# One Trainium2 core, a hybrid attention layer with 32 experts: half of the second matrix's columns computed from split weights, with the products of each unit in another order

## The chip, the cores and the metric

One core of one Trainium2 chip runs the whole layer as one program. The metric is device time in microseconds, from the first to the last instruction with what lies around them; a kernel's number is the median of its runs. PE stands for TensorE, PEld for its weight loads, DVE for VectorE, ACT for ScalarE, POOL for GpSimd, SP for SyncE.

## The reference, cut to what matters

The layer normalises 1024 tokens of width 1024, runs two kinds of attention heads, adds the result to the tokens, normalises again and sends each token to 4 of 32 experts. Only the experts are touched by the change (and the path by which `gate2`, a row of 1024 factors, reaches them):

```python
def expert_block(args):
    xe, e = args
    gu = xe @ w_gate_up[e] + b_gate_up[e]
    g = jnp.minimum(gu[:, :D_FF], SWIGLU_LIMIT)
    u = jnp.clip(gu[:, D_FF:], -SWIGLU_LIMIT, SWIGLU_LIMIT)
    act = (u + 1.0) * (g * jax.nn.sigmoid(SWIGLU_ALPHA * g))
    return act @ w_down[e] + b_down[e]
...
y = yb[dest] * gate_sorted[:, None].astype(yb.dtype)
...
return x + gate2 * y
```

All operands are float32. `w_gate_up[e]` is 1024 x 2048, `w_down[e]` 1024 x 1024.

## The kernel before, in words

**Order of the experts.** After attention and routing (until about 739 us) a loop handles the 32 experts one by one. A table `CAPS` gives the number C of token columns of each, 200 down to 96, by the rank of its load; the order sets one of 172 first, then one of 136, then wide ones (over 128, two blocks of rows) and narrow ones (128 or fewer, one block) in turn.

**Weights.** An expert's weights come in 12 chunks of 512 x 512 (1024 KB each), all issued on SP in the order of use (`load_chunk`, L775): eight of `w_gate_up`, four of `w_down`. Gate/up chunks go into a pool of five buffers (`eraw`, `NRAW`), `w_down` chunks into one of four (`draw`, `ND`). A gate/up chunk is *split* in two halves (`split_half`, L787): ACT copies 128 x 1024 values into a rounded float32 form (the *high* part, `hb`, 12 buffers, L796), and DVE subtracts that from the raw values into bfloat16 (the *low* part, `ha`, 6 buffers of two halves, L797). The subtraction stands right behind its copy.

**Products of the gate/up part** (`first_products`, L1157). The tokens are held as high and low columns side by side (`xx`, at least 256 columns) and as bfloat16 (`xb`). A *unit* is 512 columns of weights over the whole depth, two chunks: 32 high products of max(256, 2C) columns (L1167) and 32 low products of C columns in bfloat16 (L1171). They go 16 high, 16 low (first chunk), 8 high, 8 low, 8 high, 8 low (second chunk). An expert has four units: gate, up, gate, up. After each, ACT reads the low sums with the bias (L1179), DVE adds the high sums (L1183, L1181), ACT and DVE apply the sigmoid, the limits and the product (L1197, L1198, L1207, L1208), leaving `aa`.

**Products of `w_down`** (L1212 to L1229). Raw float32 weights times raw float32 `aa`: the profile shows two PE instructions for each such product, so a chunk is 32 instructions of C columns, and an expert 128. Between the two halves of the depth, PE transposes the next expert's gathered tokens (`stage_t`, L1131), which ACT, DVE and POOL copy into `xx` and `xb` (L1148, L1149, L1150). At the end ACT writes `yT` (L1225).

**The way back.** `back` (L1231) runs one step into the next expert: PE transposes `yT`, DVE multiplies by the token's weight and `gate2` (L1239), POOL scatters the rows with addition (L1153).

**What sets the order.** PE, ACT, DVE and SP run in the order in which the program is written here. `done(c)`, called when a chunk's products are issued, releases its buffers and calls `pump`, which issues every load that has a buffer, and one half split after a gate/up chunk, two after a `w_down` chunk, at most 12 halves ahead (`NH`). PSUM is eight single banks taken in turn (`bank`, L1095).

**gate2** is computed early (`mod_row`, L361) and kept as a broadcast 128 x 1024 tile.

Of the kernel before, what the change touches and what calls it, by code (L numbers as in the profile page):

```python
# [9 lines left out]
F32 = mybir.dt.float32  # L10
# [48 lines left out]
ND = 4  # L59
# [7 lines left out]
TB = 2  # L67
# [6 lines left out]
NC_ = 512  # L74
# [3 lines left out]
def hybrid_layer(ctx: ExitStack, tc: tile.TileContext, x, c_t, w_ada, b_ada_t, b_ada, norm1_t, w_in,  # L78
# [11 lines left out]
    modd = dram.tile([3, D], F32, name="modd")  # L90
# [30 lines left out]
    def rsqrt_mean(*a):  # L121
# [18 lines left out]
    gate2 = consts.tile([P, D], F32, name="gate2")  # L140
# [4 lines left out]
              [(w_down, n, kh) for kh in range(2) for n in range(2)]  # L145
    NGU, NCH = 8, len(CHUNKS0)
# [37 lines left out]
    with ExitStack() as st:  # L184
        with ExitStack() as sp:
# [164 lines left out]
            def mod_row(n, acc):  # L350
# [169 lines left out]
        with ExitStack() as so:  # L520
# [139 lines left out]
            m2 = rt.tile([P, 2, KT], F32, name="m2")  # L660
            wr = rt.tile([P, KT, E], F32, name="wr")
# [101 lines left out]
            at_ = {"dma": 0, "split": 0, "use": 0, "open": 0}  # L763
            raws, held = {}, {"eraw": 0, "draw": 0}
            pools = {"eraw": (wraw, NRAW)}
# [6 lines left out]
            def kind_of(d):  # L772
                return "eraw" if d % NCH < NGU else "draw"

            def load_chunk():  # L775
                d, kind = at_["dma"], kind_of(at_["dma"])
                i, w, n, kh = CHUNKS[d]
# [3 lines left out]
                raws[d] = pools[kind][0].tile([P, 4, NC_], F32, name=kind, bufs=pools[kind][1])  # L781
                nc.sync.dma_start(raws[d], w[ds(e, 1), kh * 512:(kh + 1) * 512, n * NC_:(n + 1) * NC_]
                                  .rearrange("o (k p) n -> p (o k) n", p=P))
                held[kind] += 1
                at_["dma"] += 1

            def split_half():  # L787

                t = at_["split"]
                c, q = t // 16 * NCH + t % 16 // 2, t % 2  # L790
                raw = raws[c][:, 2 * q:2 * q + 2]
                h_ = slot(False).rearrange("p (k n) -> p k n", k=2)
                if q == 0:
                    parts[c] = [], slot(True).bitcast(BF16).rearrange("p (k n) -> p k n", k=4)
                l_ = parts[c][1][:, 2 * q:2 * q + 2]
                nc.scalar.activation(h_, raw, AF.Copy)  # L796
                nc.vector.tensor_tensor(l_, raw, h_.bitcast(F32), OP.subtract)  # L797
                parts[c][0].extend((h_[:, j], l_[:, j]) for j in range(2))
                if q:
                    raws.pop(c)  # L800
                    held["eraw"] -= 1
                at_["open"] += 1
                at_["split"] += 1

            def pump(more):

                limit = min(at_["split"] + more, E * 16)
                while True:
                    d, t = at_["dma"], at_["split"]
                    kind = kind_of(d)  # L810
                    if d < len(CHUNKS) and kind in pools and held[kind] < pools[kind][1]:
                        load_chunk()
                    elif t < limit and t // 16 * NCH + t % 16 // 2 < d and at_["open"] < NH:
# [209 lines left out]
            pump(SPL[0] - at_["split"])  # L1023
# [6 lines left out]
            pump(SPL[1] - at_["split"])  # L1030
            pump(SPL[2] - at_["split"])
# [3 lines left out]
            pump(SPL[3] - at_["split"])  # L1035
            cur.places()
            pump(SPL[4] - at_["split"])
            cur.listed()
            pump(SPL[5] - at_["split"])
            cur.scattered()  # L1040
            pump(SPL[6] - at_["split"])
# [378 lines left out]
```

## Time and profile before

| | |
|---|---|
| runs | 2163.01 to 2168.81 us, median 2164.36 (3 runs) |
| the profiled execution | 2167.32 us, its span 2165.5 us |
| busy in the span | PE 97%, PEld 90%, DVE 69%, ACT 53%, POOL 20% |
| granted TensorE clock | 0.989 over the span |
| loads of expert weights | 256 of `eraw`, 128 of `draw`, 1024 KB each |

The experts' stage, 739 to 2153 us, is two thirds of the span, and all that follows concerns it but for a few lines. A busy PE says little by itself, since its matmuls overlap; how long a run of products takes is read from the start of one run to the start of the next in the timeline, and whether PE waited for anything from the list of waits.

### The profile page before, as it was taken

What the parts mean: (1) busy time and instruction counts of PE and PEld (TensorE: products, weight loads), DVE (VectorE), ACT (ScalarE), POOL (GpSimd) and SP (SyncE); (2) the same over time, 40 slices, a digit from 0 to 9 for tenths busy, and PEclk for the clock granted to TensorE, in tenths of its full rate; (3) what the DMA queues carried; (4) which work ended last, traced back from release to release, by engine and by line L of the source; (5) the groups of instructions that cost most, each with busy time, mean ns of one, the idle gap of its engine ahead of it and who ended that gap; (6) DMA issues with size and microseconds to landing.
All of it is one profiled execution on the core that took longest, in us unless ns stands there. A gap on an engine that the chain in (4) does not pass through costs nothing. (4 is left out here: it accounts for less than half of the span.)

```text
span 2165.5 us, 43655 instructions
## 1 busy us (share of the span) xinstructions
PE 2094.8 (97%) x16922; PEld 1957.5 (90%) x16922; DVE 1499.6 (69%) x2946; ACT 1150.2 (53%) x2263; POOL 429.3 (20%) x444
## 2 busy tenths in 40 slices
PE   7999999999999699999999999999999999999997
PEld 6877778998777699999999999999999999999997
DVE  6587756776666876677667677776767767667763
ACT  3522224777633455566456565656556656656652
POOL 2255532111045401111011111110111101101100
PEclk9999999999999799999999999999999999999999
DMA  7267886442224598799799999989989989999882
GB/s 294 73 163 215 221 230 172 114 109 76 89 105 153 192 356 299 247 334 350 255 292 326 300 314 319 332 312 343 315 297 312 361 297 320 323 315 335 297 320 60
DMA packets 272404, 548.98 MB, mean 254 GB/s; under 512 B 30675, under 2 KB 30691, under 8 KB 272067
## 3 DMA queue, kind: packets, MB, share of 16 engines
q1 hardware_dynamic: 250323, 490.09, 65.4%
q0 software_dynamic: 21872, 56.08, 11.1%
q8 instruction: 134, 2.20, 0.4%
q14 instruction: 75, 0.61, 0.1%
HBM read 501.31 MB, written 44.77 MB: 252 GB/s over the span
## 5 line engine op out<-in xcount | busy, mean ns | idle before, releaser
L797 DVE TENSOR_TENSOR ha<-eraw,hb 128x1024 bf16<-128x1024 f32 x512 | 601.3, 1224 | 233.5 <-ACT hb L796 233.0
L1167 PE MATMUL gu<-xx,hb 128*128 128x256 f32 (+13 forms) x4096 | 641.5, 304 | 0.6 <-DVE xx L1149 0.6
L1167 PEld LDWEIGHTS gu<-xx,hb 128*128 128x128 f32 x4096 | 561.1, 190 | 1.0 <-DVE xx L1149 0.8
L796 ACT ACTIVATE hb<-eraw 128x1024 fp32r<-128x1024 f32 x512 | 506.7, 1053 | 34.1 <-DMA eraw<-in_w_gate_up_dram 34.0
L1220 PE MATMUL gu<-aa,draw 128*128 128x128 f32 (+19 forms) x4096 | 521.2, 288 | 0.0
L1220 PEld LDWEIGHTS gu<-aa,draw 128*128 128x128 f32 x4096 | 511.2, 191 | 0.6
L1171 PE MATMUL gu<-xb,ha 128*128 128x128 bf16 (+19 forms) x4096 | 316.2, 224 | 0.0
L1179 ACT ACTIVATE tb<-gu,bcol 128x128 f32<-128x128 f32 (+19 forms) x512 | 164.6, 371 | 253.8 <-PE gu L1171 225.7
L1171 PEld LDWEIGHTS <-ha 128*128 128x128 bf16 x4096 | 246.6, 98 | 28.4 <-issue 3.3
L1153 POOL DMA_INDIRECT out_dram<-y,slot x47 | 81.6, 1736 | 528.3 <-DVE y L1239 251.4
L1126 POOL DMA_INDIRECT xg<-h2d,slot x47 | 54.5, 1160 | 629.0 <-PE gu L1146 381.8
L1225 ACT ACTIVATE yT<-gu,bcol 128x128 f32<-128x128 f32 (+19 forms) x256 | 82.4, 374 | 126.6 <-PE gu L1220 126.5
L572 DVE CUSTOM_DVE_ANT_0 p<-pss,bias 128x1024 f32<-128x1024 f32 (+7 forms) x128 | 94.4, 755 | 49.5 <-ACT p L581 22.2
L606 PE MATMUL po<-vsb,pT 128*128 128x64 f32 (+1 forms) x864 | 111.1, 275 | 2.6 <-ACT pT L600 1.5
L606 PEld LDWEIGHTS po<-vsb,pT 128*128 128x128 f32 x864 | 105.6, 194 | 4.8 <-ACT pT L600 1.8
L581 ACT ACTIVATE p<-p,mn 128x1024 f32<-128x1024 f32 (+7 forms) x128 | 98.6, 773 | 12.8 <-DVE mn L572 12.1
L1197 ACT ACTIVATE sg<-gt 128x256 f32<-128x256 f32 (+19 forms) x128 | 55.8, 436 | 89.2 <-DVE gt L1183 89.2
L461 PE MATMUL pp<-wh,hb 128*128 128x512 f32 x240 | 101.7, 424 | 0.0
L1198 DVE TENSOR_TENSOR gt<-gt,sg 128x256 f32<-128x256 f32 (+19 forms) x128 | 57.4, 448 | 63.4 <-ACT sg L1197 63.4
L112 POOL TENSOR_TENSOR rrs<-vrs,nhalf 128x8 f32<-128x8 f32 (+2 forms) x48 | 66.6, 1386 | 165.3 <-DVE vrs L110 160.2
L463 PE MATMUL pp<-wl,hb 128*128 128x512 f32 x240 | 94.9, 395 | 0.0
L462 PE MATMUL pp<-wh,hb 128*128 128x512 f32 x240 | 94.8, 395 | 0.0
(265 smaller groups left out, 2623.6 us busy)
## 6 DMA issues: line engine op xcount, KB each, us to landing
eraw<-in_w_gate_up_dram SPq DMA_DIRECT2D x256, 1024.0 KB
draw<-in_w_down_dram SPq DMA_DIRECT2D x128, 1024.0 KB
wraw<-in_w_ada_dram SPq DMA_DIRECT2D x32, 512.0 KB
wraw<-in_w_in_dram SPq DMA_DIRECT2D x23, 512.0 KB
hb<-in_w_ada_dram SPq DMA_DIRECT2D x16, 512.0 KB
qd<-tt POOLq DMA_DIRECT2D x32, 256.0 KB, 4.0
kd<-tt POOLq DMA_DIRECT2D x32, 256.0 KB, 4.2
ha<-qd SPq DMA_DIRECT2D x32, 256.0 KB
```

Source lines behind the costliest of these rows:

```text
L461: nc.tensor.matmul(pp, hh[b][:, k], wh[:, kk], start=(k == 0), stop=False)
L462: nc.tensor.matmul(pp, hl[b][:, k], wh[:, kk], start=False, stop=False)
L463: nc.tensor.matmul(pp, hh[b][:, k], wl[:, kk], start=False, stop=(k == KT - 1))
L572: nc.vector.tensor_tensor_reduce(p[:, :n], pss[:, :n], bias[:, (NB - 1 - ib) * P:(NB - 1 - ib) * P + n], -1.0, 3.0e38, OP.add, OP.min, mn)
L581: nc.scalar.activation(p, p, AF.Exp, bias=self.mn[c], scale=-1.0, accum_out=self.l[:, c:c + 1])
L606: nc.tensor.matmul(self.po[:, :w], self.pT[:, k], vsb[self.br][:, k, self.h * w:(self.h + 1) * w], start=(k == 0), stop=(k == self.ib))
L796: nc.scalar.activation(h_, raw, AF.Copy)
L797: nc.vector.tensor_tensor(l_, raw, h_.bitcast(F32), OP.subtract)
L1167: nc.tensor.matmul(pg[j][:, :max(256, 2 * C)], w[k][0][:, j * P:(j + 1) * P], xx[4 * kh + k], start=(kh + k == 0), stop=False)
L1171: nc.tensor.matmul(pg[j][:, C:2 * C], w[k][1][:, j * P:(j + 1) * P], xb[:, 4 * kh + k], start=False, stop=(kh == 1 and k == 3))
L1179: nc.scalar.activation(t, p[:, C:2 * C], AF.Identity, bias=bias, scale=1.0)
L1220: nc.tensor.matmul(p, w[:, k, j * P:(j + 1) * P], a[:, 4 * kh + k], start=(kh + k + j % 2 == 0), stop=(kh == 1 and k == 3 and j % 2 == 1))
```

## The change

Of the four `w_down` chunks of an expert the two of the first 512 output columns stay raw float32 (*plain*), and the two of the other 512 columns are split like gate/up chunks and computed as a fifth unit, with `a` itself as high, low and bfloat16 operands (`ax`, `ab`). So an expert has 20 half splits where it had 16. Split chunks share a ring of six buffers, plain ones have two. In each unit all 32 high products now come ahead of all 32 low ones, and the high parts' buffers are released ahead of the low ones'. The low part of a half is subtracted one half later than its copy. How many halves are split by each of the 14 steps of an expert is written out in `TG`. The transposes of the next expert's tokens stand in two places, after each plain chunk. PSUM is taken in four tiles of two banks. `gate2` is multiplied into the results while they are still transposed, as a column per partition (`g2c`), so that the way back is one ACT copy with the token's weight; it is loaded through a fourth row of `modd`. The diff, cut to its core:

```diff
-ND = 4
+NRING = 6
+NPL = 2
+TG = (12, 14, 16, 17, 19, 20, 22, 23, 24, 26, 27, 28, 28, 32)
...
-              [(w_down, n, kh) for kh in range(2) for n in range(2)]
-    NGU, NCH = 8, len(CHUNKS0)
+              [(w_down, n, kh) for n in range(2) for kh in range(2)]
+    NCH = len(CHUNKS0)
+    PLAIN = (8, 9)
...
-                    if v == 3:
-                        nc.vector.tensor_add(gate2[:, cs], pb, bb)
-                        return
                     nc.vector.tensor_add(bb, pb, bb)
...
+                nc.sync.dma_start(g2c, modd[3].rearrange("(k p) -> p k", p=P))
...
+            def low(t):
+                c, q = chunk_of(t)
+                nc.vector.tensor_tensor(parts[t][1], raws[c][:, 2 * q:2 * q + 2], parts[t][0].bitcast(F32), OP.subtract)
...
             def split_half():
...
-                nc.scalar.activation(h_, raw, AF.Copy)
-                nc.vector.tensor_tensor(l_, raw, h_.bitcast(F32), OP.subtract)
+                nc.scalar.activation(h_, raws[c][:, 2 * q:2 * q + 2], AF.Copy)
+                if t:
+                    low(t - 1)
...
-        def bank():
-            return ps4.tile([P, 512], F32, name="gu", bufs=8)
+        def banks():
+            return ps4.tile([P, 2, 512], F32, name="gu", bufs=4)
...
+        def done(high=0, low=0):
+            spent[0] += high
+            spent[1] += low
+            i, q = divmod(event[0], len(TG))
+            event[0] += 1
+            pump(i * NSP + TG[q])
...
+        def products(C, x, t0):
+            _, xb, xk = x
+            pg = [banks() for _ in range(2)]
...
             for kh in range(2):
-                c, w = take()
-                for js in ((0, 1), (2, 3)) if kh else ((0, 1, 2, 3),):
...
+                for j in range(4):
+                    for k in range(4 * kh, 4 * kh + 4):
+                        nc.tensor.matmul(pg[j // 2][:, j % 2, :max(256, 2 * C)], w[k][0][:, j * P:(j + 1) * P], xk[k],
+                                         start=(k == 0), stop=False)
                 if kh == 0:
-                    done(c)
+                    done(high=2)
+            for j in range(4):
+                for k in range(KT):
+                    nc.tensor.matmul(pg[j // 2][:, j % 2, C:2 * C], w[k][1][:, j * P:(j + 1) * P], xb[:, k],
+                                     start=False, stop=(k == KT - 1))
...
             for kh in range(2):
+                raw = raws.pop(d0 + kh)
+                for j in range(4):
+                    for k in range(4):
+                        nc.tensor.matmul(place(j), raw[:, k, j * P:(j + 1) * P], a[:, 4 * kh + k],
+                                         start=(kh + k + j % 2 == 0), stop=(kh == 1 and k == 3 and j % 2 == 1))
+                    if j == 1:
+                        f = slice(4 * kh, 4 * kh + 4)
+                        nc.scalar.activation(ah[:, f, :C], a[:, f], AF.Copy)
+                        nc.vector.tensor_sub(ah[:, f, C:], a[:, f], ah[:, f, :C].bitcast(F32))
+                        nc.gpsimd.tensor_copy(ab[:, f], ah[:, f, :C].bitcast(F32))
+                        done()
+                freed["p"] += 1
...
+                done()
+                between(kh)
+            pg = products(C, s_a, t0 + 16)
+            for j in range(4):
+                f, p = 4 + j, pg[j // 2][:, j % 2]
+                t = ap_.tile([P, 2, C], F32, name="tb", bufs=2)[:, 0]
+                nc.scalar.activation(t, p[:, C:2 * C], AF.Identity, bias=bc[:, 2 * KT + f:2 * KT + f + 1], scale=g2c[:, f:f + 1])
+                nc.vector.scalar_tensor_tensor(yT[:, f], p[:, :C], g2c[:, f:f + 1], t, op0=OP.mult, op1=OP.add)
+            done(high=2, low=4)
...
-                        nc.vector.scalar_tensor_tensor(y[:n, cs], py[:n], sl[:n, 1:2], gate2[:n, cs],
-                                                       op0=OP.mult, op1=OP.mult)
+                    nc.scalar.activation(y[:n].rearrange("p (k c) -> p k c", k=KT), py[:n], AF.Copy, scale=sl[:n, 1:2])
...
+        gate2 = fp.tile([P, D], F32, name="gate2")
+        nc.sync.dma_start(gate2, bcast_rows(modd, 3 * D, D))
```

The sums of the gate and up parts, the sigmoid and the product also go by wider tiles (two or four blocks of C columns in one DVE or ACT instruction where there were one or two).

## Rows read from the trace of the kernel before

**Rows 1.** Windows: stretch and length us; busy us of engines; clock, DMA share, GB/s.

```profile
739.20:2152.50 1413.30, 1412.65 (x13072) 1378.60 (x13072) 985.06 (x1628) 816.59 (x1503) 187.88 (x207) 1.00 0.90 307
...
1074.80:1115.70 40.90, 40.90 (x419) 40.18 (x417) 30.09 (x52) 25.30 (x48) 6.03 (x7) 1.00 0.91 294
1074.80:1198.70 123.90, 123.90 (x1235) 121.44 (x1233) 92.52 (x152) 75.52 (x142) 19.56 (x20) 1.00 0.96 311
1500.00:1520.00 20.00, 20.00 (x195) 19.66 (x195) 11.70 (x18) 10.54 (x22) 3.74 (x4) 1.00 1.05 387
```

**Rows 2.** Waits of PE in 743 to 2152 us: total, times, longest us.

```profile
PE gu L1167 <- DVE xx L1149: 0.6, 1, 0.6
```

**Rows 3.** Timeline of PE, an expert of 128 columns: start us, length us, what.

```profile
1082.31 2.15 PE L1167 MATMUL gu<-xx,hb 128*128 128x256 f32 x16
1084.31 1.07 PE L1171 MATMUL gu<-xb,ha 128*128 128x128 bf16 x16
1085.19 1.19 PE L1167 MATMUL gu<-xx,hb 128*128 128x256 f32 x8
...
1088.12 2.15 PE L1167 MATMUL gu<-xx,hb 128*128 128x256 f32 x16
...
1099.75 7.36 PE L1220 MATMUL gu<-aa,draw 128*128 128x128 f32 x64
1106.95 1.63 PE L1146 MATMUL gu<-ident,xg 128*128 128x128 f32 x16
```

**Rows 4.** The same view, an expert of 188 columns.

```profile
1028.82 2.98 PE L1167 MATMUL gu<-xx,hb 128*128 128x376 f32 x16
...
1037.07 2.98 PE L1167 MATMUL gu<-xx,hb 128*128 128x376 f32 x16
...
1053.62 10.38 PE L1220 MATMUL gu<-aa,draw 128*128 128x188 f32 x64
1063.83 1.04 PE L1146 MATMUL gu<-ident,xg 128*128 128x128 f32 x8
```

**Rows 5.** The same view, the last expert, of 96 columns.

```profile
2126.25 2.15 PE L1167 MATMUL gu<-xx,hb 128*128 128x256 f32 x16
...
2131.66 2.15 PE L1167 MATMUL gu<-xx,hb 128*128 128x256 f32 x16
...
2137.09 14.50 PE L1220 MATMUL gu<-aa,draw 128*128 128x96 f32 x128
2151.42 1.14 PE L1237 MATMUL gu<-ident,yT 128*96 128x128 f32 x8
```

**Rows 6.** Groups in 1074.8 to 1115.7 us: busy us, mean ns, idle before and releaser.

```profile
L797 DVE TENSOR_TENSOR ha<-eraw,hb 128x1024 bf16<-128x1024 f32 x16 | 18.7, 1220 | 7.7 <-ACT hb L796 7.7
...
L796 ACT ACTIVATE hb<-eraw 128x1024 fp32r<-128x1024 f32 x16 | 15.8, 1055 | 0.0
...
L1179 ACT ACTIVATE tb<-gu,bcol 128x128 f32<-128x128 f32 x16 | 5.0, 360 | 6.4 <-PE gu L1171 5.2 <-DVE ut L1181 1.2
...
L1198 DVE TENSOR_TENSOR gt<-gt,sg 128x256 f32<-128x256 f32 x4 | 1.7, 425 | 1.9 <-ACT sg L1197 1.9
...
L1239 DVE SCALAR_TENSOR_TENSOR y<-gu,slot,gate 128x512 f32<-128x512 f32 x2 | 1.4, 744 | 0.0
...
L1149 DVE TENSOR_TENSOR xx<-gu,xx 128x512 fp32r<-128x512 f32 x2 | 1.3, 686 | 1.4 <-ACT xx L1148 1.4
```

**Rows 7.** Lines 797 and 1150: shortest, median and longest instruction ns; times.

```profile
L797 DVE TENSOR_TENSOR ha<-eraw,hb x512: 1207/1219/3003, 730.2 to 2129.1; 128x1024 bf16<-128x1024 f32 x171
...
L1150 POOL CAST xb<-xx x98: 202/592/1685, 741.0 to 2106.2; 128x512 bf16<-128x512 f32 x40, 128x496 bf16<-128x496 f32 x6, 128x176 bf16<-128x176 f32 x4, 128x32 bf16<-128x32 f32 x4
```

**Rows 8.** Timelines of DVE and of POOL around 1192 us.

```profile
1191.42 4.14 DVE L797 TENSOR_TENSOR ha<-eraw,hb 128x1024 bf16<-128x1024 f32 x2
...
1192.70 1.78 POOL L1150 CAST xb<-xx 128x512 bf16<-128x512 f32 x4
```

**Rows 9.** Timeline of SP around 302 us.

```profile
302.55 0.37 SPq L618 DMA_DIRECT2D m<-modd  x1
```

More of the change, by code (lines that the diff above doesn't have):

```diff
@@ L89, in hybrid_layer @@
     ovd = dram.tile([P, 2], I32, name="ovd")
-    modd = dram.tile([3, D], F32, name="modd")
+    modd = dram.tile([4, D], F32, name="modd")
     tmp = ExitStack()
@@ L762, in hybrid_layer @@
             parts, reg = {}, {0: 0}
-            at_ = {"dma": 0, "split": 0, "use": 0, "open": 0}
-            raws, held = {}, {"eraw": 0, "draw": 0}
-            pools = {"eraw": (wraw, NRAW)}
+            at_ = {"dma": 0, "split": 0}
+            raws, pair = {}, []
+            pools = {0: (wraw, NRAW, "eraw")}
+            taken, freed = {"s": 0, "p": 0}, {"s": 0, "p": 0}
+            spent = [0, 0]
             def expert_of(i):
@@ L772, in kind_of, with room @@
             def kind_of(d):
-                return "eraw" if d % NCH < NGU else "draw"
+                return "p" if d % NCH in PLAIN else "s"
+            def room():
+                d = at_["dma"]
+                if d == len(CHUNKS):
+                    return None
+                k = kind_of(d)
+                if taken[k] - freed[k] == (NRING if k == "s" else NPL):
+                    return None
+                return pools.get("p" if k == "p" else int(taken[k] % NRING >= NRAW))
             def load_chunk():
-                d, kind = at_["dma"], kind_of(at_["dma"])
-                i, w, n, kh = CHUNKS[d]
+                d = at_["dma"]
+                pool, n, name = room()
+                i, w, c, kh = CHUNKS[d]
                 e = expert_of(i)
@@ L797, in split_half @@
-                nc.vector.tensor_tensor(l_, raw, h_.bitcast(F32), OP.subtract)
[L798 to L802, printed above, removed]
+                if t % 2 == 0:
+                    pair.append(slot(True).bitcast(BF16).rearrange("p (i k n) -> p i k n", i=2, k=2))
+                parts[t] = h_, pair[-1][:, t % 2]
+                nc.scalar.activation(h_, raws[c][:, 2 * q:2 * q + 2], AF.Copy)
@@ L803, in split_half, with pump @@
+                if t:
+                    low(t - 1)
                 at_["split"] += 1
-            def pump(more):
-                limit = min(at_["split"] + more, E * 16)
+                if t == E * NSP - 1:
+                    low(t)
+            def pump(upto):
                 while True:
-                    d, t = at_["dma"], at_["split"]
-                    kind = kind_of(d)
-                    if d < len(CHUNKS) and kind in pools and held[kind] < pools[kind][1]:
+                    if room():
@@ new lines, in expert, with joined @@
+        def expert(i, st, between):
+            C, bc = st["C"], st["bc"]
+            a = ap_.tile([P, KT, C], F32, name="ay")
+            s_a = operand(C, "ax", "ab")
+            t0, d0 = i * NSP, i * NCH + PLAIN[0]
+            def joined(dst, p, f, more):
+                t = ap_.tile([P, 2, C], F32, name="tb", bufs=2)
+                for j in range(2):
+                    nc.scalar.activation(t[:, j], p[:, j, C:2 * C], AF.Identity, bias=bc[:, f + j:f + j + 1], scale=1.0)
+                if more:
+                    nc.vector.scalar_tensor_tensor(dst, t, more, p[:, :, :C], op0=OP.add, op1=OP.add)
+                else:
+                    nc.vector.tensor_add(dst, p[:, :, :C], t)
@@ L1231, in back @@
+            pg = products(C, s_a, t0 + 16)
[4 more added lines that the diff above has]
+                nc.vector.scalar_tensor_tensor(yT[:, f], p[:, :C], g2c[:, f:f + 1], t, op0=OP.mult, op1=OP.add)
+            done(high=2, low=4)
             def back():
-                for (t0, n), sl in zip(st["blocks"], st["slots"]):
+                for (r0, n), sl in zip(st["blocks"], st["slots"]):
@@ L1309, in hybrid_layer @@
             nxt = stage_g(i + 1) if i + 1 < E else None
[L1310 removed]
+            expert(i, st, lambda g: nxt and stage_t(nxt, g))
             st = nxt
```

187 lines of the change are left out of this document (77 added, 110 removed).

## The prediction, made from the rows above

> **What bounds the kernel now.** I read the windows first: in the experts' stage PE is busy for 1412.65 of 1413.30 us while DVE is busy for 985 and ACT for 817, at the full granted clock [rows 1]. As busy matmuls overlap, I then read the waits: from 743 us on PE waited for another engine once, for 0.6 us [rows 2]. So the stage is as long as PE's own list of products, and the timeline gives the length of each piece from start to start [rows 3 to 5]. Last come the two things that could take PE's place: the vector engines (in a narrow expert of 40.9 us DVE is busy 30.1 us and ACT 25.3) and the transfers (a mean share of 0.90 at 307 GB/s over the stage, 0.96 at 311 GB/s in a stretch of three experts of at most 140 columns) [rows 1].
>
> **What PE loses and gains.** An expert gives up half of its plain instructions, 64, and gets one more unit, 32 high and 32 low products. At 128 columns the 64 plain ones take 1106.95 - 1099.75 = 7.20 us and a unit 1088.12 - 1082.31 = 5.81 us: 1.39 us saved [rows 3]. At 188 columns it is 10.21 against 8.25, 1.96 saved [rows 4]. In the last expert, 96 columns, half of 2151.42 - 2137.09 is 7.17 and a unit 5.41: 1.76 saved [rows 5]. The plain products do not get shorter below 128 columns (7.20 and 7.17) while the unit does, and above 128 they grow faster than it does. Reading all 32 experts so, from the first (1.18 us) to the last (1.76), gives 1.2 to 2.0 us each and 48 us in all: **-48**, between -46 and -50 by the spread of repeated units.
>
> The order inside a unit: a run of 16 high products takes 2.00 us and one of 16 low ones 0.88, and twice both makes 5.76, while the unit of six runs took 5.81 [rows 3]. A unit now has one run of each kind instead of three, so about 0.05 less in each of 5 x 32 units, if a run of 32 is twice one of 16. Not all of that need come: **-4**, between 0 and -10. The transposes only change place: the same number, 0.
>
> **What the evacuation must now keep up with.** The last up unit's results (`a`, second half) used to be covered by two plain chunks and the transposes, 7.2 + 1.6 us, and now by one chunk, 3.6 us, and some 0.4 us of transposes. What must fit in: two more ACT readings of 0.36, then two DVE sums and their limits and products of about 0.43 each [rows 6], some 2 us after the unit's end. With up to two half splits of 1.2 us queued ahead on DVE it takes 4.4 us at worst, so I take 0 and keep +0.5 x 32 = +16 as the bound. The fifth unit's operand costs two ACT copies, two DVE subtractions (0.69 us each by the nearest row, 128x512) and two POOL casts [rows 6, 7], the first pair under the plain products, the second half a chunk and the transposes before it is used, with 2 us of high products of the first half behind that: 0. Behind each of these on its queue stand the next half splits, which have at least one unit in hand by `TG`.
>
> PSUM as four tiles of two banks: where the expert before had two blocks of rows (17 experts, 15 of them followed by a narrow one), the gate unit and the two blocks' transposes use all four tiles, and the up unit needs the gate unit's first tile at once. That tile is free after two ACT readings and a DVE sum of two blocks (0.43 by the 256-column row) [rows 6]; its low products end 0.88 us before the unit does. ACT has the last readings of the fifth unit (0.4), four half splits (0.99 us each) and now also two copies of y ahead of it (1024 columns too, so 1.0 each) [rows 6]: 6.4 us of work in the 7.4 us that gate unit and transposes take. I take 0.2 us x 15 = **+3**, bounds 0 and +22 (1.5 us each, when ACT comes a split late).
>
> **The vector engines' load** in the narrow expert [rows 1, 6]: DVE 30.1 us, plus 4 splits of 1.17 (4.7), minus the way back (two blocks here, 2.8), plus the two subtractions (1.4), plus four sums of the fifth unit (1.0, as each is half as wide as the 0.43 of 256 columns), minus 0.9 for sums and products in half as many, twice as wide instructions: 33.5 of about 39.5 us. ACT: 25.3 + 4.0 + 1.1 + 2.0 (y) = 32.4. Both fit. But DVE also waited 11.0 us in that expert (7.7 for the copy of the half it was to subtract, 1.9 and 1.4 for others), and 33.5 + 11.0 does not fit. The change puts each subtraction one half behind its copy, so that the 7.7 us should go; then 33.5 + 3.3 = 36.8. I take **+3** for the places where it is tight.
>
> The casts on POOL bear on this. Where four of them, 1.78 us, ran beside a subtraction, that one took 3003 ns against a median of 1219, and elsewhere a cast took 1685 instead of 592 [rows 7, 8]. [...] But the mean of the subtractions in the narrow expert, 1220 ns, hardly differs from the median [rows 6, 7]: they seldom met so far, and I leave it within the +3.
>
> **Transfers.** The same bytes in less time: 311 GB/s at a share of 0.96 in the dense stretch becomes 321 at 0.99, as three experts save 4 of 123.9 us. 20 us at a share of 1.05 and 387 GB/s show that there is room above [rows 1]. Buffers are eight where they were nine. **+3**, bounds 0 and +36.
>
> **Start and end.** Each of the first expert's blocks is now copied at once after all transposes (about +0.5), and the sixth chunk waits for the second pool; at the end one ACT copy of 1.0 us stands for two DVE instructions of together 1.4 [rows 6], behind one DVE sum more, and a broadcast load of `gate2` is issued under the last scatter. The added early load is like the one of 0.37 us on SP [rows 9]; it waits for the last row of `modd`, and POOL gets two small writes, long before routing needs anything. Together **+2**, between -1 and +8.
>
> **Sum** against the profiled execution: 2167.3 - 48 - 4 + 3 + 3 + 3 + 2 = 2126.3. It lies 3.0 us over the median of the runs shown, so the median should come to **2123 us**, 1.9% less.
>
> **Rivals.**
> - *The ring of PSUM tiles.* PE waits for the gate unit's tile after every wide expert, 1.5 us x 15, and gets a few late `a` besides: 2123 + 22 = 2145. For it: ACT's queue there is full to within 1 us. Against: `TG` puts no split between the transposes and the readings. Chance 0.13.
> - *Transfers set the pace in the dense stretches.* If 0.96 is all that a long stretch gives, the narrow experts and those of 136 to 148 columns, some 24 of 32, keep their length: 24 x 1.5 = 36 us lost, of which 3 are in the sum: 2123 + 33 = 2156; with half of it 2140. For it: fewer buffers, share 0.96. Against: 1.05 in a stretch of 20 us, and PE does not wait now. Chance 0.15.
> - *Slower: DVE becomes the bound in narrow experts.* Its place is the queue of subtractions, its price the waits that it keeps: at 33.5 + 11.0 = 44.5 us the 15 narrow experts each take 3.6 us more than before, +54, the 17 wide ones still save some 28, with the order: 2164 + 26 = 2190. It decides from the point at which DVE keeps more than 39.5 - 33.5 = 6 us of idle time in such an expert. [...] Against it: the subtraction one half later takes away just the largest wait. Chance 0.12.
> - *PE stays the bound*, the forecast: 2109 (no stall anywhere) to 2137. Chance 0.60.
>
> **The numbers.** About 0.3%, 6.5 us, is what a measurement of this kernel can tell from no change. Faster by more: the forecast, the first rival and most of the second, 0.60 + 0.13 + 0.11 = 0.84. Slower by more: the third, less a mild form, 0.11. Within: 0.05. The range leaves out the slower case and the far ends: from 2108, every gain and no stall, to 2152, most of the transfer case.
>
> **What would show it.** In the profile after: L1220's successor with 64 instructions an expert instead of 128; a narrow expert of 39.5 us and one of 188 columns of 53; PE's waits in the stage below 15 us in total; DVE some 33 us busy in the narrow one, its wait for the split's copy mostly gone; the DMA share in the dense stretch at 0.99. The prediction is wrong if PE shows idle time of over 1 us in each expert: behind the gate unit means the ring, ahead of the fifth unit or of the second plain chunk DVE's queue, ahead of a unit with ACT waiting for `eraw` the transfers.

## The result, and the profile after

| | before | after |
|---|---|---|
| runs | 2163.01 to 2170.88 us, median 2167.80 (5 runs) | 2152.28 to 2156.82 us, median 2152.69 (5 runs) |
| ratio after/before | | 0.9936, 95% interval 0.9920 to 0.9952 |
| span of the profiled execution | 2165.5 us | 2151.5 us |

The change makes the kernel 14 to 15 us faster (13.9 by the ratio, 15.1 by the medians), where 41 us were forecast; the forecast median of 2123 us was missed by 29.7 us. The page of the profile after, from its parts 1 and 5:

```profile
PE 2042.9 (95%) x16922; PEld 1913.2 (89%) x16922; DVE 1643.5 (76%) x2831; ACT 1355.7 (63%) x2391; POOL 503.5 (23%) x473
...
L813 DVE TENSOR_TENSOR ha<-eraw,hb 128x1024 bf16<-128x1024 f32 x640 | 762.8, 1245 | 1.6 <-ACT hb L826 1.6
...
L1194 PE MATMUL gu<-ax,hb 128*128 128x256 f32 (+13 forms) x1024 | 159.1, 314 | 26.1 <-ACT ay L1262 25.7
```

DVE's wait for the copy of a half, 7.7 us in one narrow expert [rows 6], is down to 1.6 us in the whole kernel, as forecast. New is the last line: the high products of the fifth unit (`ax` is its operand) stand 25.7 us for ACT's L1262, which writes `yT`; the tile's name is `ay`, for `yT` shares a buffer with `a`. The list of PE's waits from 743 to 2152 us, which held one wait of 0.6 us before [rows 2], with total, times and longest:

```profile
PE gu L1194 <- ACT ay L1262: 25.7, 15, 1.8
PE gu L1194 <- DVE xx L1176: 3.6, 4, 2.2
PE gu L1250 <- DVE ay L1236: 1.7, 2, 1.2
...
```

Windows of the stage, of the expert of 128 columns and of the dense stretch [rows 1], with the same columns as there:

```profile
739.20:2138.00 1398.80, 1365.93 (x13067) 1340.24 (x13067) 1129.91 (x1492) 1020.95 (x1630) 262.08 (x232) 0.99 0.94 310
...
1071.40:1114.20 42.80, 41.05 (x421) 40.24 (x418) 34.55 (x47) 31.96 (x52) 8.00 (x7) 0.96 0.94 295
1071.40:1194.00 122.60, 118.50 (x1196) 115.93 (x1194) 102.82 (x138) 94.50 (x153) 22.93 (x21) 0.99 0.99 319
```

PE now idles for 33 us of the stage, the DMA share is where the forecast had it, and the narrow expert became longer, 42.8 us for 40.9. Its PE, from the timeline:

```profile
1088.45 1.96 PE L1200 MATMUL gu<-xb,ha 128*128 128x128 bf16 x32
1090.22 4.07 PE L1194 MATMUL gu<-xx,hb 128*128 128x256 f32 x32
1094.13 1.96 PE L1200 MATMUL gu<-xb,ha 128*128 128x128 bf16 x32
1095.92 3.79 PE L1250 MATMUL gu<-ay,draw 128*128 128x128 f32 x32
1099.55 0.94 PE L1172 MATMUL gu<-ident,xg 128*128 128x128 f32 x8
1100.42 3.84 PE L1250 MATMUL gu<-ay,draw 128*128 128x128 f32 x32
1104.10 0.94 PE L1172 MATMUL gu<-ident,xg 128*128 128x128 f32 x8
1104.97 1.22 PE L1194 MATMUL gu<-ax,hb 128*128 128x256 f32 x8
1107.94 4.63 PE L1194 MATMUL gu<-ax,hb 128*128 128x256 f32 x24 [1.75 <-ACT ay L1262]
1112.41 1.79 PE L1200 MATMUL gu<-ab,ha 128*128 128x128 bf16 x29
```

A unit of long runs takes 1095.92 - 1090.22 = 5.70 us, and the 32 plain instructions of a chunk 3.63. The fifth unit's high products, which take 3.91 us as the runs of 32 do elsewhere, take 1112.41 - 1104.97 = 7.44: eight, a pause, and 24 of which most are slow. Its windows show why they are slow (the granted clock is the number ahead of the last two):

```profile
1105.90:1107.90 2.00, 0.29 (x3) 0.09 (x1) 2.00 (x3) 1.52 (x5) 0.93 (x1) 1.00 0.93 315
1107.90:1108.70 0.80, 0.76 (x6) 0.77 (x7) 0.66 (x1) 0.80 (x1) 0.00 (x0) 1.00 0.97 376
1108.70:1112.00 3.30, 3.30 (x18) 3.30 (x18) 1.39 (x2) 1.19 (x3) 1.25 (x2) 0.50 1.08 348
```

PE goes on at the full granted clock (1.00) for 0.8 us after the pause, and then at one of 0.50 for 3.3 us. What PE waited for is in the timelines of DVE and ACT:

```profile
1099.97 1.22 DVE L813 TENSOR_TENSOR ha<-eraw,hb 128x1024 bf16<-128x1024 f32 x1
1101.10 0.69 DVE L1255 TENSOR_TENSOR ax<-ay,ax 128x512 fp32r<-128x512 f32 x1
1101.70 3.90 DVE L813 TENSOR_TENSOR ha<-eraw,hb 128x1024 bf16<-128x1024 f32 x3
1105.53 0.15 DVE L1165 TENSOR_TENSOR bcol<-bcol,g2c 128x8 f32<-128x8 f32 x1
1105.61 0.68 DVE L1255 TENSOR_TENSOR ax<-ay,ax 128x512 fp32r<-128x512 f32 x1
```

```profile
1101.49 0.63 ACT L1254 ACTIVATE ax<-ay 128x512 fp32r<-128x512 f32 x1
1102.01 1.06 ACT L826 ACTIVATE hb<-eraw 128x1024 fp32r<-128x1024 f32 x1
1106.38 1.50 ACT L1262 ACTIVATE ay<-gu,bcol,g2c 128x128 f32<-128x128 f32 x4 [3.31 <-DVE bcol L1165]
```

ACT's copy for the second operand half is done at 1102.1, but its subtraction (L1255) stands on DVE behind three half subtractions and starts at 1105.61. It reads `a`. `yT` may be written only when nobody reads `a` any more, so ACT waits 3.31 us, though the plain products were done at 1104.26. The trace names L1165, the DVE instruction just ahead, but that one was over at 1105.68; L1262 starts at 1106.38, 0.09 us after the end of L1255. In 19 other experts it names L1255 itself; ACT's waits at this line from 743 to 2140 us:

```profile
ACT ay L1262 <- DVE ax L1255: 57.1, 19, 3.7
ACT ay L1262 <- PE gu L1250: 23.0, 7, 4.2
ACT ay L1262 <- DVE bcol L1165: 16.9, 5, 3.5
...
```

Until `yT` is written the plain results hold their PSUM tile. Where the next expert has two blocks of rows, its transposes hold two of the four tiles, and the fifth unit's second tile is that of the plain results: PE stops after the eight products of the first, and its ninth starts, here, 0.06 us after the end of L1262. The tiles are so placed in 16 experts, 14 narrow ones and the first two; only the very first, of 172 columns, shows no pause.

Start to start, summed over the 32 experts from the timeline, in us (E1 is the first experiment, below):

| | before | after | E1 |
|---|---|---|---|
| up to the first product of the experts | 742.8 | 744.4 | 746.3 |
| four gate/up units | 824.1 | 810.1 | 809.4 |
| plain products | 508.1 | 257.7 | 262.3 |
| fifth unit | | 244.0 | 201.9 |
| transposes of the next tokens | 36.9 | 40.3 | 44.8 |
| transposes on the way back | 39.6 | 39.4 | 39.4 |
| from the start of the last transposes to the end | 14.1 | 15.6 | 16.1 |
| span | 2165.5 | 2151.5 | 2120.2 |

The fifth unit is 42.1 us longer than in E1. That is more than the 29.7 us by which the forecast was missed, since other pieces came out better or worse than forecast. (The time up to the experts' first product differs by some us from profile to profile, 740.5 to 749.9 us over these runs.)

### The profile page after: what moved, and what is told of

Same layout as the page of the kernel before. It is cut to its first block, busy times and chain, and to the rows that moved or that the text cites. A ratio compares the mean times of both kernels' runs of the same rounds, so it can differ in the third digit from the quotient of the medians.

```text
span 2151.5 us, 43844 instructions
## 1 busy us (share of the span) xinstructions
PE 2042.9 (95%) x16922; PEld 1913.2 (89%) x16922; DVE 1643.5 (76%) x2831; ACT 1355.7 (63%) x2391; POOL 503.5 (23%) x473
## 4 chain that ended last, share of the span: by engine, by line
PE 45%; DVE 13%; ACT 9%; issue 6%; DMA 2%; POOL 0%; SPq 0%; ACTq 0%; POOLq 0%; DVEq 0%
PE gu L1194 25%; PE gu L1200 11%; PE gu L1250 5%; DVE ha L813 5%; ACT hb L826 4%; PE gu L1279 2%; PE po L605 1%; ACT ay L1262 1%; DMA eraw<-in_w_gate_up_dram 1%; DMA eraw<-in_w_down_dram 1%; DVE ax L1255 1%; ACT tb L1214 1%; DVE su L1235 1%; DVE su L1216 1%; DVE ixf L924 1%
## 5 line engine op out<-in xcount | busy, mean ns | idle before, releaser
L813 DVE TENSOR_TENSOR ha<-eraw,hb 128x1024 bf16<-128x1024 f32 x640 | 762.8, 1245 | 1.6 <-ACT hb L826 1.6
L826 ACT ACTIVATE hb<-eraw 128x1024 fp32r<-128x1024 f32 x640 | 634.2, 1051 | 13.4 <-DMA eraw<-in_w_down_dram 11.1
L1194 PE MATMUL gu<-xx,hb 128*128 128x256 f32 (+13 forms) x4096 | 587.7, 300 | 3.6 <-DVE xx L1176 3.6
L1200 PEld LDWEIGHTS <-ha 128*128 128x128 bf16 x5120 | 310.8, 97 | 11.9 <-issue 1.5
L1250 PE MATMUL gu<-ay,draw 128*128 128x128 f32 (+19 forms) x2048 | 267.6, 289 | 1.7 <-DVE ay L1236 1.7
L1250 PEld LDWEIGHTS gu<-ay,draw 128*128 128x128 f32 x2048 | 257.3, 191 | 2.7 <-DVE ay L1236 2.1
L1194 PE MATMUL gu<-ax,hb 128*128 128x256 f32 (+13 forms) x1024 | 159.1, 314 | 26.1 <-ACT ay L1262 25.7
L1194 PEld LDWEIGHTS gu<-ax,hb 128*128 128x128 f32 x1024 | 148.5, 203 | 30.0 <-ACT ay L1262 28.8
L1256 POOL CAST ab<-ax 128x512 bf16<-128x512 f32 (+19 forms) x64 | 68.4, 1072 | 266.8 <-ACT ax L1254 266.8
L1270 ACT ACTIVATE tb<-gu,bcol,g2c 128x128 f32<-128x128 f32 (+19 forms) x128 | 56.4, 466 | 107.7 <-PE gu L1200 77.9
L1262 ACT ACTIVATE ay<-gu,bcol,g2c 128x128 f32<-128x128 f32 (+19 forms) x128 | 49.4, 466 | 99.9 <-DVE ax L1255 57.1
```

The lines of the kernel that those rows point to most:

```text
L813: nc.vector.tensor_tensor(parts[t][1], raws[c][:, 2 * q:2 * q + 2], parts[t][0].bitcast(F32), OP.subtract)
L826: nc.scalar.activation(h_, raws[c][:, 2 * q:2 * q + 2], AF.Copy)
L1194: nc.tensor.matmul(pg[j // 2][:, j % 2, :max(256, 2 * C)], w[k][0][:, j * P:(j + 1) * P], xk[k], start=(k == 0), stop=False)
L1200: nc.tensor.matmul(pg[j // 2][:, j % 2, C:2 * C], w[k][1][:, j * P:(j + 1) * P], xb[:, k], start=False, stop=(k == KT - 1))
L1250: nc.tensor.matmul(place(j), raw[:, k, j * P:(j + 1) * P], a[:, 4 * kh + k], start=(kh + k + j % 2 == 0), stop=(kh == 1 and k == 3 and j % ...
L1262: nc.scalar.activation(yT[:, j], place(j), AF.Identity, bias=bc[:, 2 * KT + j:2 * KT + j + 1], scale=g2c[:, j:j + 1])
```

## Experiments

Ratios are to the kernel before, with 95% intervals; the kernel before had a median of 2165.9 to 2167.9 us in these sets.

| run | edit | median us | ratio |
|---|---|---|---|
| E1 | after, `yT` not in `a`'s buffer | 2122.01 | 0.9789 (0.9772 to 0.9805) |
| E2 | after, second operand half a chunk earlier | 2124.5 | 0.9798 (0.9782 to 0.9815) |
| E3 | after, without the new casts | 2136.69 | 0.9853 (0.9837 to 0.9869) |
| E4 | after, old order of runs | 2153.35 | 0.9930 (0.9914 to 0.9947) |
| E5 | E1, splits in other steps | 2120.86 | 0.9792 (0.9771 to 0.9813) |
| E6 | E1, new casts on ACT | 2119.25 | 0.9788 (0.9766 to 0.9810) |
| E7 | E1, old order of runs | 2134.4 | 0.9861 (0.9841 to 0.9881) |
| E8 | after, fifth unit tile by tile | 2133.68 | 0.9850 (0.9833 to 0.9867) |
| E9 | before, new order of runs | 2167.42 | 1.0002 (0.9992 to 1.0012) |
| E10 | E1, plain chunks loaded last | 2123.19 | 0.9795 (0.9779 to 0.9812) |
| E11 | E10 with E6's edit | 2120.54 | 0.9785 (0.9769 to 0.9802) |
| E12 | E11 with E5's edit | 2119.71 | 0.9773 (0.9757 to 0.9789) |
| E13 | before, new order, way back in its place | 2154.12 | 0.9946 (0.9934 to 0.9957) |

### E1: `yT` in buffers of its own

```diff
-                    yT = ap_.tile([P, KT, C], F32, name="ay")
+                    yT = [ap_.tile([P, 4, C], F32, name=n) for n in ("gt", "su")]
```

(and `yT[0][:, j]`, `yT[1][:, j]`, `yT[k // 4][:, k % 4]` where it is used; the buffers of `gt` and `su` are idle by then)

> Edit: the results yT no longer take the buffer of a; their halves take the buffers of gt and su, which are free by then. Nothing else moves. Theory A (chain: the second half's subtraction for the operand stands on DVE behind three half subtractions; yT shares the buffer of a, so ACT may not write yT before that subtraction; so the plain chunks' PSUM tile stays taken, and the fifth unit, which takes that tile where the next expert has two blocks, stops for 2 us and then runs at half clock): the high runs of the fifth unit in narrow experts fall from 5.8 to 7.5 us to about 3.9 to 4.3, PE's wait for L1262 goes (25.7 us), granted clock back to 0.989, time about 2152.7 - 38 = 2115 us. Rival B (the subtraction is too late for the fifth unit itself): a pause of 1 us or more stays at the unit's second half of the depth, time 2135 to 2150. Rival C (ACT's own queue is too long, so that yT is late with or without the shared buffer): less than 10 us gained, 2143 or more.

The pause is gone. The same place in E1, PE and then ACT, and PE's waits from 743 us on:

```profile
1097.71 0.94 PE L1172 MATMUL gu<-ident,xg 128*128 128x128 f32 x8
1098.59 4.06 PE L1194 MATMUL gu<-ax,hb 128*128 128x256 f32 x32
1102.49 1.96 PE L1200 MATMUL gu<-ab,ha 128*128 128x128 bf16 x32
```

```profile
1097.91 1.51 ACT L1262 ACTIVATE gt<-gu,bcol,g2c 128x128 f32<-128x128 f32 x4 [1.18 <-PE gu L1250]
```

```profile
PE gu L1250 <- DVE ay L1236: 6.6, 6, 2.0
PE gu L1194 <- DVE xx L1176: 2.2, 1, 2.2
...
```

ACT now waits for the plain products and not for DVE, and the fifth unit takes 3.90 + 1.77 us. DVE's list around it is the same as above, three half subtractions of together 3.90 us ahead of the second L1255: the operand itself was in time all along. The whole gain of 30.7 us over the changed kernel comes from a buffer that was shared. It is 7 us short of theory A's 2115 us; what is left in PE's list is in the main the wait for `ay` written by L1236, that is for `a`.

### E2 and E3: the two other ends of the wait

E2 makes the second operand half at the end of the first plain chunk, so that its subtraction comes before the three halves:

```diff
-                    if j == 1:
-                        f = slice(4 * kh, 4 * kh + 4)
+                    if kh == 0 and j % 2:
+                        f = slice(2 * j - 2, 2 * j + 2)
...
```

> Edit: the second half of the fifth unit's operand (copy, subtraction, cast) is issued at the end of the first plain chunk, ahead of the two half splits there, instead of in the middle of the second one. The buffer stays shared. Theory A: the subtraction ends some 3 to 4 us earlier, yT waits for PE alone, and the pause goes: 2112 to 2120 us. Rival B: also gone, so this run does not tell A from B. Rival C (ACT's queue): no change, 2150, or worse, as ACT then waits for a.

E3 leaves the buffer and the order, and takes the two casts per expert away; zeros stand for the bfloat16 operand of the fifth unit:

```diff
...
-                        nc.gpsimd.tensor_copy(ab[:, f], ah[:, f, :C].bitcast(F32))
...
```

> Edit: the 64 new casts on POOL are left out; the low products of the fifth unit read a tile of zeros, so the low part of that half of w_down is missing from the result. Theory D (the casts hold the half subtractions on DVE, whose mean rose from 1224 to 1245 ns, and so make the second operand subtraction late): the mean falls back to about 1225, the subtraction comes 0.6 us or more earlier, the pause is shorter by that much in 15 experts and the half clock follows it less often: 2130 to 2143 us. If the casts do not matter: 2150 to 2154.

E2's list of PE's waits has no wait for the writing of `yT` at all (L1263 there). In E3 it is still there, though shorter:

```profile
PE gu L1194 <- ACT ay L1262: 17.3, 15, 2.0
```

```profile
L813 DVE TENSOR_TENSOR ha<-eraw,hb 128x1024 bf16<-128x1024 f32 x640 | 744.9, 1217 | 1.9 <-ACT hb L826 1.9
```

So either end will do, the buffer or the place of the subtraction in DVE's queue. The casts make a third of the pause (and, with what follows it, 16 us of the time), but they are not its cause. They do hold the subtractions up: a mean of 1217 ns without them and 1245 with them, 28 ns x 640 = 18 us of DVE, which bears on the time only through that queue.

### E4, E7, E9 and E13: the order of the runs

E4 puts the order of before (16 high, 16 low, then 8 by 8) into the kernel after, E7 into E1:

```diff
-                for j in range(4):
...
+                for js in ((0, 1), (2, 3)) if kh else ((0, 1, 2, 3),):
+                    for j in js:
...
```

> Edit: in each unit the products go back to the order 16 high, 16 low, 8 high, 8 low, 8 high, 8 low, all else as in the changed kernel. Theory E (long runs save about 0.13 us in each unit of a narrow expert, 14.0 us over the four gate and up units by the timelines of both kernels and 17 with the fifth): 2152.7 + 14 to 18 = 2167 to 2171, the four units of a 128-column expert at 23.3 us instead of 22.8. If the gain has another cause (PSUM in tiles of two banks, wider sums): 2150 to 2156.

> Edit on top of e1: the products of each unit in the order 16 high, 16 low, 8, 8, 8, 8 again. In e4 the four units did get 14.0 us longer and the time did not, as the fifth unit's pause got shorter by 13.6. Theory E (the long runs are worth 14 us in the four units and 3 in the fifth): without that pause they show in full, 2122 + 14 to 18 = 2136 to 2140 us. Rival (the order also moves the sums, and one pays for the other): 2120 to 2128 us.

E4's four units take 824.2 us again, 14 more, and yet its time is that of the kernel after, so that it fell where the rival cause was expected. It pauses less:

```profile
PE gu L1195 <- ACT ay L1263: 16.7, 15, 1.4
```

Its fifth unit takes 228.1 us for 244.0, although the old order makes its own products 5.1 us longer (207.0 us in E7 for 201.9 in E1). The idle time is 9.0 us less (16.7 for 25.7): part of what the runs save in the changed kernel is waited away a few us later, where DVE's queue sets the end of the pause and not PE. Some 11 us more come from the clock, which stays at 1.00 in E4 from 760 to 2125 us and fell to 0.50 behind seven pauses of the kernel after. The stage itself is 3.4 us shorter in E4; its experts start 3.8 us later. In E7, without the pause, the old order costs 2134.4 - 2122.0 = 12.4 us (15.6 by the ratios, as the two were timed in different sets), a little less than expected. The four units take 13.5 us more (823.0 for 809.4) and the fifth 5.1; the plain products and the next tokens' transposes take 8.5 less, where PE's waits for `a` are 1.9 us instead of 6.6.

E9 and E13 put the new order into the kernel before. In E9 both chunks of a unit are released together at its end, and with that the transposes on the way back, which run at the first release of an expert, moved from inside the gate unit to behind it. E13 leaves them after the first 16 high products:

```diff
                                          start=(kh + k == 0), stop=False)
+                if kh == 0:
+                    steps()
...
-            done(cw[0][0])
+            done(cw[0][0], False)
```

> The kernel before with one edit: in each unit all 32 high products ahead of all 32 low ones (both chunks released at the unit's end). Theory: the order alone is worth about 14 us in the four gate/up units (824 us summed over the experts become 810) and nothing else in the kernel before is near PE, so 2167 becomes 2153, ratio 0.993 to 0.9945, with PE's waits in the stage still below 3 us. Rival A: the order only looks better in the changed kernel, since there wide tiles of PSUM and the later subtraction go with it: units 820 to 824, time 2163 to 2168. Rival B: chunk buffers released later make the next halves late: units shorter, but new PE waits for hb or ha of over 10 us, time 2160 to 2175.

> The kernel before with the long runs of e9, but with the transposes on the way back left inside the gate unit, after its first 16 high products, as both kernels of this case have them (e9 had moved them behind the gate unit, and lost there what the runs gave). Theory: the shorter runs cost what the timeline shows, 0.13 us a unit at 128 columns and 0.08 at 188, so the four units take 810 to 813 us instead of 824, nothing else moves, ratio 0.993 to 0.996, time 2153 to 2159. Rival: the order's gain needs the tiles of two banks too; with single banks the up unit waits for the gate unit's sums wherever the transposes stand: units 817 to 824 us, time 2162 to 2168.

E9 gains nothing, for a reason that none of its theories named. Its timeline at the place:

```profile
1079.76 1.92 PE L1237 MATMUL gu<-ident,yT 128*128 128x128 f32 x16
1081.74 4.62 PE L1166 MATMUL gu<-xx,hb 128*128 128x256 f32 x32
1086.20 1.96 PE L1171 MATMUL gu<-xb,ha 128*128 128x128 bf16 x32
```

```profile
1080.94 2.71 DVE L1239 SCALAR_TENSOR_TENSOR y<-gu,slot,gate 128x512 f32<-128x512 f32 x4
1083.58 0.47 DVE L1183 TENSOR_TENSOR gt<-gu,tb 128x128 f32<-128x128 f32 x2
```

The up unit behind the transposes takes 1086.20 - 1081.74 = 4.46 us for its high products instead of 3.91, and from the start of the transposes to its own start it is 1.98 us instead of 1.67. One by one in the trace, its first products on its four banks start at 1081.74, 1082.40, 1083.05 and 1083.71, each 0.055 us after DVE has read one of the transposes' four banks (L1239 ends at 1081.68, 1082.34, 1082.99 and 1083.65). It is so in all 15 narrow experts behind one of two blocks. So the up unit gets the banks of the transposes, which DVE empties one in 0.66 us. The gate unit's banks, which it would get if the eight were taken strictly in turn, are read only later (L1183 from 1083.58), and PE does not wait for that. All this stands in no list of waits: the longest idle time of PE there is 0.06 us in the trace, as the modelled length of a matmul covers the rest; only start-to-start times show it. With the transposes back inside the gate unit (E13) DVE is ahead of the up unit, and the order gives 12.9 us, 0.9946: the four units take 813.2 us for 824.1, 10.9 less, and in the profiled executions 2.2 us lie ahead of the experts' stage; PE waits 2.4 us in the stage. So the order has its worth alone, with single banks too. E9 is of the same kind as the forecast's first rival, an up unit that waits for PSUM, though for the transposes' banks and not for the gate unit's.

### E8: the fifth unit one tile after the other

The high products of the fifth unit go tile by tile, 16 on the first instead of eight, so that the second is needed eight products, about 1 us, later; the high parts' buffers are all released at the unit's end:

```diff
-            for kh in range(2):
-                for j in range(4):
+            for kh, js in ((0, (0, 1)), (1, (0, 1)), (0, (2, 3)), (1, (2, 3))) if tiles else ((0, range(4)), (1, range(4))):
+                for j in js:
...
```

> Edit of the changed kernel: in the fifth unit the high products go through the first PSUM tile in full depth and then through the second, so the second tile, that of the plain chunks, is wanted 1 us later; yT keeps the shared buffer. Theory A (PE waits for that tile): the pause of about 1.8 us becomes 0.8 us or less, too short for the lower clock, 2120 to 2132 us. Rival B (PE waits for the operand's second half): wanted 1 us earlier now, so the pause stays or grows: 2150 or more.

```profile
PE gu L1194 <- DVE ax L1255: 5.4, 12, 1.8
PE gu L1194 <- ACT ay L1262: 5.2, 15, 0.4
```

The wait for the tile shrinks from 1.8 us to at most 0.4, as it should if the tile is what PE waits for, but now the products of the second operand half come sooner, and PE meets the late subtraction itself. The wait moved a step up its own chain, and 19 us of 31 are had. That 0.8 us is "too short for the lower clock" is the author's estimate; in the kernel after, a pause of 1.24 us ahead of 1319.71 us left the granted clock at 1.00 (1320 to 1326 us).

### E5, E6, E10 to E12: what is left without the pause

```diff
-TG = (12, 14, 16, 17, 19, 20, 22, 23, 24, 26, 27, 28, 28, 32)
+TG = (12, 14, 16, 18, 20, 22, 22, 24, 25, 26, 27, 28, 28, 32)
```

```diff
-                        nc.gpsimd.tensor_copy(ab[:, f], ah[:, f, :C].bitcast(F32))
+                        nc.scalar.activation(ab[:, f], a[:, f], AF.Copy)
```

```diff
-              [(w_down, n, kh) for n in range(2) for kh in range(2)]
+              [(w_down, n, kh) for n in (1, 0) for kh in range(2)]
-    PLAIN = (8, 9)
+    PLAIN = (10, 11)
```

The first is E5, the second E6, the third E10, each on top of E1.

> Edit on top of e1: the steps of TG are 12, 14, 16, 18, 20, 22, 22, 24, 25, 26, 27, 28, 28, 32, so no half is split in the middle of the last up unit and those before it come a step earlier. What is left in e1 are waits of the second plain chunk for a (6.6 us, followed by half clock, some 12 us in all). Theory G (DVE's queue of subtractions ahead of the last up unit's sums makes a late): the waits go, 2110 to 2115 us. Theory H (a late chunk: ACT stands at a half whose transfer has not landed, and the sums behind it wait): an earlier split wants its chunk earlier, so no gain or a loss, 2120 to 2130 us.

> Edit on top of e1: the 64 casts of the fifth unit's operand are made by ACT from a, not by POOL (the low products then use a rounded once). Theory D with A (casts cost DVE time, which decides only while the second subtraction is on PE's path): the half subtractions' mean falls from 1245 to about 1225 ns, yet the time stays within 4 us of e1, 2118 to 2126 us. If the casts cost PE time in another way: 2110 or less.

> The changed kernel with yT's halves in the buffers of gt and su (as in the run e1), and of an expert's four w_down chunks the two split ones are loaded ahead of the two plain ones. Theory H: the split w_down chunks come late because in SP's list their loads stand behind plain loads that wait for one of two plain buffers; then ACT's waits for eraw filled from w_down (28.4 us in 12 pauses) fall below 5 us, PE's wait for ay written by the limits' product (6.6 us in e1) below 2 us, and the time is 2110 to 2118 against 2122. Rival: the bytes per microsecond are the limit, then another chunk is late in its place: the waits move to eraw of w_gate_up or to draw with the same sum, 2119 to 2126.

> The run before it and, in addition, the cast of the fifth unit's low operand on ACT instead of POOL, which keeps it from meeting DVE's subtractions. If the two add up: about 3 us less than the run before it (as e6 was 2.9 us below e1), 2107 to 2116, half subtractions with a mean of 1218 ns instead of 1245. Rival: ACT, with 64 more instructions, is late for its copies of the halves: 2115 to 2125.

> The run before it with three half splits a step earlier (the schedule of e5). If splits that stand behind the last sums of an expert are what PE still waits for, its waits in the stage go below 8 us and the time is 1 to 2 us lower, 2106 to 2115. Rival: no more to be had there, since e5 was within 1.3 us of e1: within 1.5 us of the run before it, 2108 to 2118.

ACT's waits for chunks of weights, in E1 and then in E10, from 700 us on:

```profile
ACT hb L826 <- DMA eraw<-in_w_down_dram: 28.4, 12, 6.4
...
ACT hb L826 <- DMA eraw<-in_w_gate_up_dram: 4.3, 3, 3.4
```

```profile
ACT hb L826 <- DMA eraw<-in_w_gate_up_dram: 19.8, 10, 6.8
```

E10 took the late `w_down` chunks away, and the waits came back at `w_gate_up`; PE's wait for `a` stayed (6.9 us for 6.6), and so did the time. The reason for which E10 was made falls. E6 brings the subtractions back to a mean of 1218 ns and lowers the median by 2.8 us, E11 lowers E10's by 2.7, E5 and E12 theirs by about one; every one of these is inside the intervals. By the ratios E5 and E6 gain nothing over E1 (0.9792 and 0.9788 for 0.9789), although PE's wait for `a` falls to 3.7 and 3.2 us in them. E6 has the lowest median, 2119.25 us, and E12 the lowest ratio, 0.9773, but from E1 neither can be told. E11 and E12 came out 4.5 and 4.7 us above their theories' ranges. That transfers are near their limit here is likely, not shown: in E1 the mean share is 1.00 over 193 us,

```profile
1107.00:1300.00 193.00, 190.67 (x1835) 187.38 (x1833) 158.32 (x207) 142.85 (x228) 36.66 (x31) 0.99 1.00 315
```

and no run changed the bytes.

## Why the prediction was wrong

**The step that failed** is "the second half a chunk and the transposes before it is used, with 2 us of high products of the first half behind that: 0". It asked when the fifth unit reads the operand, and there it was right: E1 keeps the late subtraction and PE waits for it 0.2 us. It did not ask who else waits for that subtraction. The diff gives `a` and `yT` one name, `ay`, and so one buffer: the last reader of `a` became a DVE instruction with three half subtractions ahead of it. The prediction named what stands *behind* the new instructions on their queues and not what stands ahead of them; it allowed for two half splits ahead of the last up unit's sums, and for none ahead of the operand. It also looked for the shortage of PSUM tiles at the up unit alone, and the four tiles have a second tight place, the fifth unit, where the holder is the plain chunk's result. Nearest to it came the sign it gave for DVE's queue, idle time of PE "ahead of the fifth unit"; the time was lost inside it. The price was 42.1 us, 40 of it in the 15 experts whose 32 high products took 5.7 to 7.5 us instead of 3.9 to 4.3: some 28 us are the pause, some 11 the granted clock of 0.50 behind seven of the 15 pauses (3.5 us more than in E1 where the clock fell, 1.9 where it did not).

**The products, -48:** right. With the old order and no pause (E7) the fifth unit takes 207.0 us, and it stands for half of 508.1: -47.

**The order of the runs, -4:** mis-sized. The change measured -14.0 in the four units (824.1 to 810.1), E13 -10.9 in them and -12.9 in the time, and the fifth unit has another 5.1 (207.0 in E7, 201.9 in E1). The bound was -10. The text took a run of 32 as twice one of 16: 2 x 2.00 = 4.00, but it takes 3.91. The trace of the kernel before had the answer: 16 high products took 2.00 [rows 3] and eight 1.03, as the row behind the eight at 1085.19 shows:

```profile
1086.22 0.62 PE L1171 MATMUL gu<-xb,ha 128*128 128x128 bf16 x8
```

So each start of a high run has a price of its own, 0.06 to 0.09 us by these numbers (2 x 1.03 - 2.00 and 2 x 2.00 - 3.91), while low runs (0.43, 0.88 and now 1.77) have hardly any. One run of each kind for three saves 0.12 us a unit at 128 columns (the four units of that expert take 22.82 us for 23.31). The rebate "not all of that need come" had no row behind it.

**The transposes, 0, and `a` late, 0 with a bound of +16:** the transposes of the next tokens and the plain products stand 3.4 and 3.7 us above the forecast in the kernel after, and 7.9 and 8.2 in E1 (the sums above; half of 508.1 for the plain ones). In the kernel after only 1.7 us of this are waits for `a`, and the clock stays at 1.00 around them; most of the rest is that one run became two: 16 transposes take 1.74 us for 1.56 in the expert of 128 columns, and its 64 plain instructions 7.31 for half of 14.37. "The transposes only change place" left that out. In E1 PE is early enough to wait 6.6 us for `a`, and behind two of these waits the granted clock is 0.50 (from 1136.8 and from 1310.9 us).

**PSUM at the up unit, +3:** 0; no such wait is in the list, and the units behind the transposes are no longer than the others start to start, which E9 shows to be the safer sign. **DVE, +3:** the busy times were right (34.55 and 31.96 us in the narrow expert against 33.5 and 32.4), the subtraction one half later took its wait away, and the slower case, in which DVE keeps its waits, did not come. **Transfers, +3:** 0.99 and 319 GB/s in the dense stretch against 0.99 and 321 forecast, and PE waits for no load there. **Start and end, +2:** 1.7 + 1.5. **The median:** the 3.0 us taken off for it had no ground in the end, as the kernel before has a median of 2167.80 us over five runs.

E1's 2122.01 us is the forecast's 2123 almost to the us. That is luck and no merit of the sum: the order gave some 16 us more there than was forecast, and the plain products and the next tokens' transposes lost 16 that the sum did not have. E1 is also another kernel than the one that was forecast.

**DVE's order and the casts.** The three half subtractions and L1255 ran in the order in which they were issued, although L1255's input was there 3.5 us before it started (ACT's copy ends at 1102.1 us, L1255 starts at 1105.61): whoever adds an instruction to DVE here has to count what is ahead of it. The prediction left the meetings of casts and subtractions within its +3 for DVE. Without the casts on POOL (E3 and E6) a subtraction takes 1217 and 1218 ns in the mean against 1245: the casts cost 18 us of DVE's time, of which 3 us at most reach the end in E6, where the pause is gone.

## What to carry to other kernels

When a change gives one more instruction a tile to read, list everything that waits for the last reader of that tile: the next writer of its buffer, and whoever needs the buffers that this writer sets free. Count what is queued ahead of the new instruction on its engine as well as behind it. And when a local gain does not show in the time, look for a pause a few us later whose end is set by another engine: it can swallow a gain ahead of it, as it did here with part of what the order of the runs saves (E4), and most of that shows once the pause is gone (E7).

## What the hardware showed that was not expected

Seven of the 15 pauses, which kept PE from its next product for 1.8 to 2.1 us, were followed by 14 to 17 products at a granted clock of 0.50, 213 ns from start to start for 120; the other eight were not (1.00 from 1014.7 to 1018.0 us, behind an idle time of 1.76 us). So a pause of 2 us cost 2 us at one time and 3.5 at another. In E4, with pauses of at most 1.4 us, the clock behind them stayed at 1.00. But in E3 a pause of 1.25 us was followed by 17 products at 0.50:

```profile
934.16 4.63 PE L1194 MATMUL gu<-ax,hb 128*128 128x256 f32 x24 [1.25 <-ACT ay L1262]
```

```profile
934.50:937.80 3.30, 3.30 (x18) 3.30 (x17) 1.63 (x3) 1.59 (x3) 1.22 (x2) 0.50 1.03 388
```

So the length of a pause alone does not tell, in these runs, whether the clock falls behind it.

The pauses of E9 were in no list of waits, and cost 0.8 us in each narrow expert, against E13: in E9 the up unit's banks came free 0.66 us apart, PE counted as busy but for at most 0.06 us at a time, and only the distances between starts tell.
